# A macaron transformer block: the mixer's input projections in sets of seven block products

## The chip, the cores and the metric

One Trainium2 chip, one core. The time is the device time of one execution in microseconds (us); a profiled execution gives its span, from the first to the last instruction, on that core. The engines: PE (TensorE, matrix products), ACT (ScalarE), DVE (VectorE), POOL (GpSimd), and SP (SyncE), which issues DMA transfers. Each engine works through its own queue in order.

## The reference, cut to what matters

512 tokens, width 1024, float32 in and out.

```python
x = x + 0.5 * swiglu(rmsnorm(x, g1), w_gu1, w_down1)          # d_ff 2816
x = x + hybrid_mixer(rmsnorm(x, gm), ...)
x = x + 0.5 * swiglu(rmsnorm(x, g2), w_gu2, w_down2)
return rmsnorm(x, gf)

def hybrid_mixer(h, ...):
    cb, cc, cu, q, k, v, g_lr, r, ga, gb = split(h @ w_in)    # 3x1024, 2x512, 1024, 16, 3x1024
    y_conv = (cb * causal_short_conv(cc * cu, conv_w)) @ w_out_conv
    log_a = log_sigmoid(g_lr @ gate_w_up + gate_b) / 16
    o = gla_chunked(q, k, v, log_a)                           # 4 heads, chunks of 64 tokens
    o = o * rsqrt(mean(o * o) + eps) * gla_norm_g
    y_gla = (o * silu(r)) @ w_out_gla
    return (sigmoid(ga) * y_conv + sigmoid(gb) * y_gla) @ w_o
```

## The kernel before, in words

Activations lie transposed: 8 tiles `x[k]` of 128 features by 512 tokens. Every float32 operand of a large product is split into a rounded part h and the remainder l (type float32r), and a product is three passes on PE: h*h, h*l, l*h. A weight unit of 128 x 1024 arrives in an `f` buffer by an SP transfer (L254); ACT casts it to `wh` (L279), and DVE subtracts to get `wl` (L280). `PLAN` lists the weight units, `STEPS` their order; `Weights.take` issues casts two steps ahead of use, and `fetch` starts loads `early` steps ahead.

A plain column tile (`mm_single`, L307 to L309) is 8 k tiles x 3 passes = 24 matmuls of 512 columns. `mm_group` does four column tiles with k outermost, `mm_wide` four token tiles of v.

In both FFNs most up columns go instead by sets (`Set`, L469): two columns of 256 by 512 tokens and 1024 inputs, taken as 2 x 2 blocks, need seven block products and not eight, at the price of sums. The seven are called m1, p2, q6, p5, q7, p4, p3. Four weight units of a set are summed among themselves: one sum by DVE (L267), three by transfers that add, on POOL's queue (L258, `f<-f`). `Operands.make` builds the seven sums and differences of the normed input once per FFN, with scratch tiles `bf` and two rings, `opA` (8 tiles) and `opB` (6). Products collect in three PSUM banks a set; ACT copies the bank after m1, q6 and q7 (L474), before the next product goes into the same bank; DVE combines the results. `order` interleaves neighbouring sets.

The mixer uses no sets. It works on x times the norm's gain and scales by the norm's row at each evacuation: q and k of heads 0 and 1 (group), q and k of heads 2 and 3, then the gating of all four heads in one go (`gates`, `decays`, `qk_scale`: Abs, Exp, Ln, scan, Exp, then multiplies on DVE and POOL) around the two halves of v, then per head state and output between the 24 convolution tiles, then 8 tiles of r, 8 of ga with 8 of w_out_conv, 8 of gb with 8 of w_out_gla, and w_o. Everything lives in a pool `tp` of 50 tiles; `f` has 4 buffers there, and 10 in an FFN. As soon as `x[d]` is final, `Norm.add` splits it and adds up its squares; `Norm.finish` sums over partitions on PE (L413, L414) and makes the row.

`last_down` produces the output with tokens on partitions: 20 of 22 k tiles for all eight outputs (four token tiles by two halves), then per output the last two, followed by the residual, squares, final norm and store (L705 to L738); multiplying by the final gain is POOL's (L443 from `part`).

The order of instructions on each engine is set by a planner that goes by modelled costs and readiness; where the code says `manual_schedule` it is the order written. When a phase ends, its tiles' memory is given to the next phase's, and a new tile waits for the last use of the old ones under it.

Of the kernel before, what the change touches and what calls it, by code (L numbers as in the profile page):

```python
# [38 lines left out]
ODD_FILL = 272  # L39

# [69 lines left out]

def ffn_plan(up, down, plain, slow):
# [5 lines left out]
    firsts = []  # L117
    for s in range(plain // 2, KF // 2):
        firsts.append(len(PLAN))
        PLAN.extend((up, 4 * j, 4, (i * DFF + s * HW,), HW) for i in range(2) for j in range(2))  # L120
    STEPS.extend(order(firsts))
    units(full(down, KF))
    ENDS.append(len(STEPS))


def mixer_plan():
    units(group("w_in", KD, (QO, KO, QO + P, KO + P)))
    for h in (2, 3):
        units(single("w_in", KD, QO + h * P))
        units(single("w_in", KD, KO + h * P))  # L130
    units(wide("w_in", KD, VO))
    units(wide("w_in", KD, VO + 512))
    for j in range(KD):
        for c in (CC, CU, CB):
            units(single("w_in", KD, c + j * P))
    for j in range(KD):
        units(single("w_in", KD, RO + j * P))
    for d in range(KD):
        units(single("w_in", KD, GA + d * P))
        units(single("w_out_conv", KD, d * P))  # L140
    for d in range(KD):
        units(single("w_in", KD, GB + d * P))
# [18 lines left out]
def block_kernel(ctx: ExitStack, tc: tile.TileContext, xT, vecs, gf, gup, wgl, wts, out):  # L161
# [48 lines left out]
    X = keep.tile([P, KD, S], F32, tag="X", name="X")  # L210
    x = [X[:, k] for k in range(KD)]
    for n, b in (("wh", 3), ("wl", 3), ("opA", 8)):
        pools[n] = ctx.enter_context(tc.tile_pool(name=n, bufs=b))
    acc_row = ctx.enter_context(tc.tile_pool(name="acc_row", bufs=1))
    class Weights:
# [13 lines left out]
        def phase(self, early):  # L229
# [4 lines left out]
            for i in range(lo, self.end):  # L234
                n, p = STEPS[i]
                if p == "m1":
                    self.loads.setdefault(max(lo, i - 6), []).append(n)
# [22 lines left out]
        def issue(self):  # L260
# [16 lines left out]
            h = tile_of("wh", [P, 1024], F32R)  # L277
            l = tile_of("wl", [P, 1024], F32R)
# [58 lines left out]
    def mm_wide(mat, kt, col, ah, al):  # L337
        o = [MM() for _ in range(NTB)]
        for u in wide(mat, kt, col):
            h, l = W.take(u)  # L340
            for i in range(u[2]):
# [3 lines left out]
                for t in range(NTB):  # L345
# [4 lines left out]
                    nc.tensor.matmul(o[t], b, wh, start=False, stop=k == kt - 1)  # L350
        return o
# [8 lines left out]
    def halves(dtype):  # L360
        t = tile_of("opA", [P, 1024], dtype)
# [116 lines left out]
    class Operands:  # L478
# [3 lines left out]
        def __init__(self, b, nk):  # L482
            self.b = b
            self.nk = nk
            self.parts = {}
            self.f = {}

        def split(self, p, v):
            n = self.nk * HW
            h, l = (tile_of("opB" if p in ("m1", "p2", "q6") else "opA", [P, 1024], F32R)  # L490
                    for _ in range(2))
            hv, lv = (t[:, :n].rearrange("p (k t) -> p k t", t=HW) for t in (h, l))
# [4 lines left out]
        def new(self):  # L497
            t = tile_of("bf", [P, 1024])
            return t[:, : self.nk * HW].rearrange("p (k t) -> p k t", t=HW)

        def make(self, p):
            if p in self.parts:
                return
            b, f = self.b, self.f
            if p == "q6":
                f["D1"] = self.new()
                nc.vector.tensor_tensor(out=f["D1"], in0=b(0, 0), in1=b(0, 1), op=ALU.subtract)
                f["D2"] = self.new()
                nc.vector.scalar_tensor_tensor(out=f["D2"], in0=b(1, 1), scalar=-1.0, in1=f["D1"],
                                               op0=ALU.mult, op1=ALU.subtract)  # L510
            if p == "q7":
                f["T3"] = self.new()
                nc.vector.tensor_tensor(out=f["T3"], in0=b(1, 1), in1=b(0, 1), op=ALU.subtract)
            if p == "p4":
                f["T4"] = self.new()
                nc.vector.scalar_tensor_tensor(out=f["T4"], in0=f["D2"], scalar=-1.0, in1=b(1, 0),
                                               op0=ALU.mult, op1=ALU.subtract)
            v = {"m1": lambda: b(0, 0), "p2": lambda: b(1, 0), "q6": lambda: f["D2"],
                 "p5": lambda: f["D1"], "q7": lambda: f["T3"], "p4": lambda: f["T4"],
                 "p3": lambda: b(1, 1)}[p]()  # L520
            self.split(p, v)

# [3 lines left out]
    def run_sets(make, ahead=2):  # L526
# [6 lines left out]
        for i, n in enumerate(sets):  # L533
            sets[n] = make(i)
        for i, (n, p) in enumerate(seq):
            for n_, p_ in seq[i : i + ahead + 1]:
                sets[n_].group.make(p_)
            sets[n].run(p)


    def ffn(up, down, norm, nxt, plain, at):
# [25 lines left out]
        xo = Operands(normed, 4)  # L567
# [57 lines left out]
        def split_hid(k):  # L625

            h, l = (tile_of("opB", [P, 2, S], F32R) for _ in range(2))
# [31 lines left out]
    def natural(i):  # L659

        o = AUX()
# [4 lines left out]
    def last_down(us, split_hid):  # L666
        gr = []
        for e in range(2):
            g = tile_of("bf", [P, 1024])[:, :512]
# [12 lines left out]
        for k in range(KF - 2):  # L682
# [6 lines left out]
        w = [W.take(u) for u in us[KF - 2 :]]  # L689
        hl = split_hid(KF - 2)  # L690
# [8 lines left out]
        def part(t, e):  # L699

            s0, s1, b0, v, r, q = fin[t]
            for i in range(2):
                mm(t, e, KF - 2 + i, w[i], hl)
# [3 lines left out]
            nc.scalar.activation(blocks(T()), xt, AF.Square, accum_out=s1 if e else s0)  # L707
            y = T()
            ys[t].append(y)
            mul(blocks(y), xt, blocks(gr[e]), nc.gpsimd)  # L710
            if e == 0:
                nc.scalar.activation(b0, s0, AF.Copy, scale=1.0 / D, bias=EPS)
            else:
                nc.scalar.activation(r, s1, AF.Sqrt, scale=1.0 / D, bias=b0)

        def rstd(t):
            s0, s1, b0, v, r, q = fin[t]
            nc.vector.scalar_tensor_tensor(out=v, in0=s1, scalar=1.0 / D, in1=b0,
# [6 lines left out]
            if t != last:  # L725
                mul(r, r, q)

        def store(t, e):
            s0, s1, b0, v, r, q = fin[t]
            xt = ys[t][e]  # L730
            if t == last:
                nc.vector.tensor_scalar(out=xt, in0=xt, scalar1=r, scalar2=q,
                                        op0=ALU.mult, op1=ALU.mult)
            elif e:
                nc.vector.tensor_scalar(out=xt, in0=xt, scalar1=r, scalar2=None, op0=ALU.mult)
            else:
                nc.scalar.activation(xt, xt, AF.Copy, scale=r)
            nc.sync.dma_start(out[t, e], xt)  # L738

        with tc.manual_schedule(engines={ENG.PE, ENG.DVE, ENG.Activation, ENG.Pool}):  # L740

            early = front.tile([P, 1], F32, tag="early", name="early")
            nc.scalar.activation(early, hl[1][:, 1, 0:1].bitcast(F32), AF.Square)
            nc.scalar.activation(early, early, AF.Sqrt)
            for t in range(NTB):
# [12 lines left out]


    def mixer(norm, nxt):  # L760
        xh, xl = norm.h, norm.l
        cpool = pools["small"]

        maskf = cpool.tile([P, P], F32, tag="maskf", name="maskf")
        mask = cpool.tile([P, P], I32, tag="mask", name="mask")
        nc.gpsimd.memset(maskf, 1.0)
# [5 lines left out]
        upad = []  # L772
        for i in range(2):
            u = cpool.tile([P, S + 2], F32, tag=f"upad{i}", name=f"upad{i}")
            nc.gpsimd.memset(u[:, :2], 0.0)
            upad.append(u)
        gl_raw = cpool.tile([P, KD, RANK], F32, tag="glraw", name="gl_raw")
        nc.sync.dma_start(gl_raw, wgl)
        gl_w = cpool.tile([P, KD, 3, 2 * RANK], F32R, tag="glw", name="gl_w")
        cpool.tile([P, ODD_FILL], F32, tag="fill", name="odd_fill")  # L780
        reset = T()
        nc.gpsimd.memset(reset, 1.0)
        nc.gpsimd.memset(reset.rearrange("p (c t) -> p c t", t=CH)[:, :, 0:1], 0.0)
        sc = []
        for i in range(2):
            s = T()
            nc.gpsimd.memset(s, 0.0)
            sc.append(s)


        nc.vector.tensor_copy(gl_w[:, :, 0, :RANK], gl_raw)
        nc.vector.tensor_tensor(out=gl_w[:, :, 0, RANK:], in0=gl_raw,
                                in1=gl_w[:, :, 0, :RANK].bitcast(F32), op=ALU.subtract)
        for i in (1, 2):
            nc.gpsimd.tensor_copy(gl_w[:, :, i], gl_w[:, :, 0].bitcast(F32))
# [12 lines left out]
        def gate_k(k):  # L808
            if k == 2:
# [335 lines left out]
```

## Time and profile before

| | us |
|---|---|
| median of 3 runs (lowest, highest) | 1240.21 (1239.68, 1240.63) |
| profiled execution | 1239.92 |
| its span | 1238.2 |
| busy PE / DVE / ACT / POOL | 1219.9 / 691.0 / 493.3 / 116.9 |
| first FFN, mixer, second FFN, roughly | 0 to 352, 352 to 870, 870 to 1238 |

A line such as `L307 ... x480 | 188.3, 392 | 0.0` gives engine, operation, output and inputs, count, busy us, mean ns of one, and idle time of the engine before them with its cause. Matmuls overlap, so their mean length is not their spacing. Times in a timeline or chain are start and length from the start of the span.

### The profile page before, as it was taken

The page shows a single profiled execution, that of the slowest core. Times are in us where ns is not written, and L with a number is a line of the kernel's source. Part 1 is how long each engine was busy: PE and PEld are TensorE (multiplying, and loading weights), DVE is VectorE, ACT ScalarE, POOL GpSimd, SP SyncE. Part 2 cuts the span into 40 slices and gives each one's busy share as a digit, 9 for nine tenths or more (in the row PEclk, how much of TensorE's full clock was granted, in tenths as well). Part 3 has the DMA queues.
Part 4 walks back from the last instruction along what each step waited for, and adds up shares of the span by engine and source line. Part 5 has one row for each costly group of instructions (what it writes and reads, how often), then busy time and mean ns, then how long its engine had stood idle before and what let it go on. Part 6 is the DMA issues. An engine that isn't in the chain of part 4 may idle for free.

```text
span 1238.2 us, 16644 instructions
## 1 busy us (share of the span) xinstructions
PE 1219.9 (99%) x6874; PEld 1070.5 (86%) x6874; DVE 691.0 (56%) x817; ACT 493.3 (40%) x628; POOL 116.9 (9%) x131
## 2 busy tenths in 40 slices
PE   9999999999999999999999999999899999999996
PEld 8899999888878788888888888888689999998885
DVE  7976666532374764444584334445587656563325
ACT  6555445422252722222344222223355545452233
POOL 0011110000010251100011000000001111100003
PEclk9999999999999999999999999999899999999998
DMA  9477776631232223222223333330648777753201
GB/s 340 105 185 191 177 191 170 165 95 34 70 92 85 85 85 86 82 72 86 85 85 102 97 91 102 102 91 30 238 101 202 177 185 175 183 171 88 66 1 68
DMA packets 42748, 149.75 MB, mean 121 GB/s; under 512 B 4944, under 2 KB 5072, under 8 KB 42672
## 3 DMA queue, kind: packets, MB, share of 16 engines
q1 hardware_dynamic: 34752, 120.34, 30.5%
q0 software_dynamic: 7776, 28.32, 13.1%
q8 instruction: 54, 0.88, 0.3%
q14 instruction: 22, 0.18, 0.0%
q10 hardware_dynamic: 144, 0.03, 0.0%
HBM read 118.26 MB, written 2.10 MB: 97 GB/s over the span
## 4 chain that ended last, share of the span: by engine, by line
PE 94%; DVE 2%; ACT 1%; DMA 1%; issue 1%; POOL 0%; DVEq 0%; ACTq 0%; POOLq 0%
PE mm L469 27%; PE mm L307 14%; PE mm L308 14%; PE mm L309 14%; PE mm L331 7%; PE mm L679 2%; PE mm L678 2%; PE mm L680 2%; PE mm L349 1%; DMA f<-f 1%; PE aux L309 1%; PE aux L307 1%; PE aux L308 1%; PE mm L350 1%; PE mm L348 1%
## 5 line engine op out<-in xcount | busy, mean ns | idle before, releaser
L279 ACT CAST wh<-f 128x1024 fp32r<-128x1024 f32 (+1 forms) x275 | 287.4, 1046 | 599.0 <-PE mm L308 238.0
L280 DVE TENSOR_TENSOR wl<-f,wh 128x1024 fp32r<-128x1024 f32 (+1 forms) x275 | 337.2, 1229 | 262.3 <-ACT wh L279 260.2
L469 PE MATMUL mm<-opA,wh 128*128 128x256 f32 x1152 | 210.0, 283 | 1.3 <-ACT tp L474 1.3
L307 PE MATMUL mm<-opA,wh 128*128 128x512 f32 x480 | 188.3, 392 | 0.0
L308 PE MATMUL mm<-opA,wh 128*128 128x512 f32 x480 | 187.6, 391 | 0.0
L309 PE MATMUL mm<-opA,wl 128*128 128x512 f32 x480 | 187.0, 390 | 0.0
L469 PEld LDWEIGHTS mm<-opA,wh 128*128 128x128 f32 x1152 | 179.8, 192 | 1.8 <-ACT tp L474 1.7
L469 PE MATMUL mm<-opA,wl 128*128 128x256 f32 x576 | 163.0, 283 | 0.0
L469 PE MATMUL mm<-opB,wh 128*128 128x256 f32 x864 | 158.1, 284 | 0.0
L469 PEld LDWEIGHTS mm<-opB,wh 128*128 128x128 f32 x864 | 134.8, 192 | 0.2
L469 PE MATMUL mm<-opB,wl 128*128 128x256 f32 x432 | 122.2, 283 | 0.0
L469 PEld LDWEIGHTS mm<-opA,wl 128*128 128x128 f32 x576 | 110.6, 192 | 0.0
L309 PEld LDWEIGHTS mm<-opA,wl 128*128 128x128 f32 x480 | 90.2, 188 | 18.7
L308 PEld LDWEIGHTS mm<-opA,wh 128*128 128x128 f32 x480 | 90.1, 188 | 18.4
L307 PEld LDWEIGHTS mm<-opA,wh 128*128 128x128 f32 x480 | 90.1, 188 | 18.4
L258 POOL DMA_DIRECT2D f<-f x54 | 46.6, 863 | 603.4 <-DVE f L267 294.1
L469 PEld LDWEIGHTS mm<-opB,wl 128*128 128x128 f32 x432 | 82.9, 192 | 0.0
L443 DVE TENSOR_TENSOR tp<-mm,tp 128x512 f32<-128x512 f32 x36 | 24.8, 691 | 102.5 <-PE mm L309 101.8
L307 PE MATMUL mm<-tp,wh 128*128 128x512 f32 x160 | 62.2, 389 | 0.0
L308 PE MATMUL mm<-tp,wh 128*128 128x512 f32 x160 | 62.2, 389 | 0.0
L309 PE MATMUL mm<-tp,wl 128*128 128x512 f32 x160 | 62.2, 389 | 0.0
L678 PE MATMUL mm<-wh,opB 128*128 128x512 f32 x132 | 51.4, 389 | 0.0
(204 smaller groups left out, 1700.2 us busy)
## 6 DMA issues: line engine op xcount, KB each, us to landing
f<-wts SPq DMA_DIRECT2D x219, 512.0 KB, 3.9
f<-f POOLq DMA_DIRECT2D x54, 512.0 KB, 4.8
X<-xT SPq DMA_DIRECT2D x8, 256.0 KB, 5.3
y<-tp SPq DMA_DIRECT2D x8, 256.0 KB, 2.1
f<-wts SPq DMA_DIRECT2D x2, 256.0 KB, 3.5
bf<-gf SPq DMA_DIRECT2D x2, 256.0 KB, 4.3
tp<-gup SPq DMA_DIRECT2D x6, 32.0 KB, 1.8
gl_raw<-wgl SPq DMA_DIRECT2D x1, 64.0 KB, 4.2
```

The lines of the kernel that those rows point to most:

```text
L258: nc.gpsimd.dma_start(out_, a, accum_op=ALU.add)
L279: nc.scalar.copy(h[:, :w], raw[:, :w])
L280: nc.vector.tensor_tensor(out=l[:, :w], in0=raw[:, :w], in1=h[:, :w].bitcast(F32), op=ALU.subtract)
L307: nc.tensor.matmul(o, wh, ah, start=first, stop=False)
L308: nc.tensor.matmul(o, wh, al, start=False, stop=False)
L309: nc.tensor.matmul(o, wl, ah, start=False, stop=last)
L331: nc.tensor.matmul(o[c], w[:, s : s + P], a[k], start=k == 0 and j == 0, stop=k == kt - 1 and j == 2)
L443: (eng or nc.vector).tensor_tensor(out=out_, in0=a, in1=b, op=ALU.mult)
L469: nc.tensor.matmul(to, ww[:, s], aa[:, t], start=fresh and k == 0 and e == 0 and j == 0, stop=k == 3 and j == 2, skip_group_check=True)
L678: nc.tensor.matmul(o[t][e], a, wh, start=k == 0, stop=False)
L679: nc.tensor.matmul(o[t][e], a, wl, start=False, stop=False)
L680: nc.tensor.matmul(o[t][e], b, wh, start=False, stop=k == KF - 1)
```

## The change

1. **Mixer by sets.** cc, cu, cb, r, ga and gb (48 column tiles) become 12 sets; q, k and v stay plain, in the order group, half of v, q and k of heads 2 and 3, other half of v. The input is multiplied by the norm's gain and row in place (`normed`), so nothing is scaled at evacuation.
2. **Heads one at a time.** Gating, scores, state, output and squares of heads 0 and 1 run between the plain tiles, of 1 to 3 in hooks between products of the first six sets. All of it is on PE, ACT and DVE; POOL no longer multiplies.
3. **Memory.** x goes to DRAM at the mixer's start and returns near its end; the gates, after Sigmoid, go to DRAM by transfers on ACT's queue and return by SP's. Buffers `f`: 10 in all phases; `tp`: 6 in the mixer, 9 in an FFN.
4. **One ring** `op` of 14 tiles replaces `opA`, `opB` and `bf`; the operand sums are formed in place, one after the other (m1, p2, p5, q6, q7, p4, p3). The last two tiles of w_o are both multiplied before either is evacuated.
5. **Tail.** The last four k tiles (`TAIL`) are taken output by output; POOL's multiply moves to DVE, one store of the last tile to ACT's queue.

```diff
+TAIL = 4
+MSETS = [("ga", 0), ("gb", 0), ("conv", 0), ("ga", 1), ("conv", 1), ("gb", 1), ("conv", 2),
+         ("conv", 3), ("cb", 0), ("cb", 1), ("r", 0), ("r", 1)]
...
     units(group("w_in", KD, (QO, KO, QO + P, KO + P)))
+    units(wide("w_in", KD, VO))
     for h in (2, 3):
         units(single("w_in", KD, QO + h * P))
         units(single("w_in", KD, KO + h * P))
-    units(wide("w_in", KD, VO))
     units(wide("w_in", KD, VO + 512))
-    for j in range(KD):
-        for c in (CC, CU, CB):
-            units(single("w_in", KD, c + j * P))
-    for j in range(KD):
-        units(single("w_in", KD, RO + j * P))
+    base = {"ga": GA, "gb": GB, "cb": CB, "r": RO}
+    sets("w_in", [(CC + i * HW, CU + i * HW) if n == "conv" else
+                  (base[n] + 2 * i * HW, base[n] + (2 * i + 1) * HW) for n, i in MSETS])
...
-    for n, b in (("wh", 3), ("wl", 3), ("opA", 8)):
+    for n, b in (("wh", 3), ("wl", 3), ("op", 14)):
...
+            late = at >= len(STEPS) - TAIL
+            h = tile_of("op" if late else "wh", [P, 1024], F32R)
+            l = tile_of("op" if late else "wl", [P, 1024], F32R)
...
+        hooks = {
+            (0, "m1"): [lambda: scores(1)], (0, "q6"): [lambda: state(1)],
+            (0, "q7"): [lambda: output(1)], (0, "p4"): [lambda: squares(1)],
+            (0, "p3"): [move],
+            (1, "q6"): [lambda: gates(2)], (1, "q7"): [decays], (1, "p4"): [lambda: scale(2)],
+            (2, "q6"): [lambda: scores(2)], (2, "q7"): [lambda: state(2)],
+            (2, "p4"): [lambda: output(2)], (3, "q6"): [lambda: squares(2)],
+            (3, "q7"): [lambda: gates(3)], (3, "p3"): [decays], (4, "q6"): [lambda: scale(3)],
+            (4, "p3"): [lambda: scores(3)], (5, "q6"): [lambda: state(3)],
+            (5, "p4"): [lambda: output(3)], (5, "p3"): [lambda: squares(3)],
+        }
...
+                gates_d[name][d : d + 2, :, half(l)].rearrange("e p t -> p e t"), pair(t))
...
+        def gate(name, d):
+            t = T()
+            nc.sync.dma_start(t, gates_d[name][d])
+            return t
...
-        for d in range(4, KD):
+        for d in range(4, KD - 2):
             evac(d, mm_single("w_o", KD, d * P, m_h, m_l))
+        for d, o in [(d, mm_single("w_o", KD, d * P, m_h, m_l)) for d in range(KD - 2, KD)]:
+            evac(d, o)
...
-    FFN = dict(f=10, opB=6, hid=11, bf=2, tp=6)
+    FFN = dict(f=10, hid=11, tp=9)
...
-    with phase("small2", f=4, small=1, tp=50):
-        W.phase(2)
+    with phase("small2", f=10, tp=6, v=4, qk=2, g=1, y=4, small=1):
+        W.phase(4, 5)
```

In the new tail, `part(t, e, acc)` does the four k tiles of an output, its residual, squares and gain; `rstd(t)` and `store(t)` follow a token tile later:

```diff
-        for k in range(KF - 2):
+        for k in range(KF - TAIL):
...
-            for i in range(2):
-                mm(t, e, KF - 2 + i, w[i], hl)
+            for i in range(TAIL):
+                mm(t, e, KF - TAIL + i, w[i], hl[i // 2])
...
-            mul(blocks(y), xt, blocks(gr[e]), nc.gpsimd)
+            mul(blocks(ys[t][e]), xt, blocks(gr[e]))
...
+            (nc.scalar if t == last else nc.sync).dma_start(out[t, 1], ys[t][1])
```

More of the change, by code (lines that the diff above doesn't have):

```diff
@@ L116, in ffn_plan @@
         units(single(up, KD, DFF + f * P))
[L117 to L121, printed above, removed]
+    sets(up, [(s * HW, DFF + s * HW) for s in range(plain // 2, KF // 2)])
     units(full(down, KF))
@@ L495, in split, with run_sets @@
             self.parts[p] = (h, l)
[L497 to L521, printed above, removed]
         def get(self, p):
             return self.parts[p]
-    def run_sets(make, ahead=2):
+    def run_sets(make, ahead=2, hooks={}):
         at = W.taken
@@ L532, in run_sets @@
         sets = {n: None for n, _ in seq}
-        for i, n in enumerate(sets):
+        number = {n: i for i, n in enumerate(sets)}
+        for n, i in number.items():
             sets[n] = make(i)
@@ new lines, in mixer, with normed @@
+        for h in range(2):
+            evac_q(h, qk[2 * h])
+            evac_k(h, qk[2 * h + 1])
+        X = XS[-1]
+        done_k = set()
+        def normed(j, l):
+            for k in range(4 * j, 4 * j + 4):
+                if k not in done_k:
+                    done_k.add(k)
+                    nc.vector.scalar_tensor_tensor(
+                        out=x[k], in0=x[k], scalar=vec[:, norm.goff + k : norm.goff + k + 1],
+                        in1=row, op0=ALU.mult, op1=ALU.mult)
+            return X[:, 4 * j : 4 * j + 4, l * HW : (l + 1) * HW]
@@ new lines, in v_half, with one, extra @@
+        def v_half(i, extra=None):
+            for t, o in enumerate(mm_wide("w_in", KD, VO + 512 * i, xh, xl, extra)):
+                nc.scalar.copy(vt[i][t], o)
+        def one(fs):
+            def extra(k):
+                for f in fs.get(k, ()):
+                    f()
+            return extra
+        v_half(0, one({1: [lambda: gates(0)], 3: [decays], 5: [lambda: scale(0)]}))
+        oq = mm_single("w_in", KD, QO + 2 * P, xh, xl)
+        scores(0)
+        evac_q(2, oq)
+        ok = mm_single("w_in", KD, KO + 2 * P, xh, xl)
@@ new lines, in mixer, with move @@
+        state(0)
+        evac_k(2, ok)
+        xo.make("m1")
+        oq = mm_single("w_in", KD, QO + 3 * P, xh, xl)
+        output(0)
+        evac_q(3, oq)
+        ok = mm_single("w_in", KD, KO + 3 * P, xh, xl)
+        squares(0)
+        gates(1)
+        evac_k(3, ok)
+        xo.make("p2")
+        v_half(1, one({1: [decays], 3: [lambda: scale(1), lambda: xo.make("p5")],
+                       5: [lambda: xo.sum("q6")]}))
+        OB = []
+        def move():
+            OB.append(big("O").rearrange("p (h e) t -> p h e t", e=2))
+            for h in range(2):
+                nc.scalar.copy(OB[0][:, h], O[h])
+            for h in range(HEADS):
+                O[h] = OB[0][:, h]
+            for i in range(4):
+                nc.gpsimd.memset(Y[i][:, :, :2], 0.0)
@@ new lines, in cb_done, with done @@
+        def cb_done(i):
+            def done(s, p):
+                bank, v = s.bank, s.v
+                y = [Y[2 * i + a][:, :, 2:] for a in range(2)]
+                if p == "p4":
+                    c = y[1][:, :, half(0)]
+                    nc.vector.scalar_tensor_tensor(out=c, in0=pair(bank["b"]), scalar=-1.0, in1=c,
+                                                   op0=ALU.mult, op1=ALU.mult)
+                    return
+                t = quarter(s, p)
+                if t is not None:
+                    c = y[p == "q7"][:, :, half(p != "p2")]
+                    mul(c, pair(t), c)
+            return done
@@ new lines, in r_done, with use, f, make @@
+        def r_done(i):
+            def use(a, l, t):
+                def f():
+                    o = O[2 * i + a][:, :, half(l)]
+                    mul(o, o, pair(t))
+                late.append(f)
+            return act_done(AF.Silu, use)
+        kinds = {"ga": lambda i: gate_done("ga", i), "gb": lambda i: gate_done("gb", i),
+                 "conv": conv_done, "cb": cb_done, "r": r_done}
+        def make(n):
+            name, i = MSETS[n]
+            f = kinds[name](i)
+            def done(s, p):
+                if p in ("p2", "p5", "q7", "p4", "p3"):
+                    finish_late()
+                f(s, p)
+            return Set(xo, done)
@@ L1052, in mixer @@
+        c_h, c_l = parts([Y[i][:, :, 2:] for i in range(4)])
+        m = [two(d // 2)[:, d % 2] for d in range(KD)]
+        n64 = [front.tile([P, HEADS * 16], F32, tag=t, name=f"{t}o") for t in
+               ("st_v", "st_s", "st_r")]
+        r64, s64, q64 = n64
+        newton_rsqrt(r64, vs, s64, q64)
+        og = []
         for d in range(KD):
-            gp = mm_single("w_in", KD, GA + d * P, xh, xl)
-            t = T()
-            mul(t, gp, row)
-            nc.scalar.activation(t, t, AF.Sigmoid)
+            t = gate("ga", d)
```

569 lines of the change are left out of this document (309 added, 260 removed).

## The prediction

> **What bounds the kernel now.** I read the page first: busy shares (part 1), then the chain that ended last by engine (part 4).
>
> ```profile
> span 1238.2 us, 16644 instructions
> PE 1219.9 (99%) x6874; PEld 1070.5 (86%) x6874; DVE 691.0 (56%) x817; ACT 493.3 (40%) x628; POOL 116.9 (9%) x131
> ...
> PE 94%; DVE 2%; ACT 1%; DMA 1%; issue 1%; POOL 0%; DVEq 0%; ACTq 0%; POOLq 0%
> ```
>
> PE is busy 99% and carries 94% of the chain. So this change can win in three ways only: less matmul time, shorter holes in PE, a shorter end after PE. The sum goes against the profiled execution: 1239.92 us, its span of 1238.2 and 1.7 around it; the median of the runs, 1240.21, is 0.3 above.
>
> **Matmul time.** The chain in order of time merges unbroken stretches, so it gives rates, where a group's mean gives overlapping lengths: first 96 matmuls of 512 columns, then the 168 of one set of 256 columns.
>
> ```profile
> 826.89 21.76 PE mm L331 x96
> ...
> 1009.88 20.15 PE mm L469 x168
> ```
>
> Four column tiles cost 96 plain matmuls (8 k tiles, 3 passes): 21.76 us, 0.2267 each. The same columns as a set are 7 products of 4 k tiles, 2 halves, 3 passes: 168 matmuls, 20.15 us, 0.1199 each. A set saves 1.61 us (7%, not 1/8, as 256 columns cost more than half of 512). 48 tiles make 12 sets: **-19.3 us**. Other matmuls stay in number: q, k, v, the three output projections, the attention. That all of this time is on the path is shown by the windows: in the mixer PE lacks 1.3 us of 518.4.
>
> ```profile
> core 0: us, PE busy (x) PEld busy (x) DVE busy (x) ACT busy (x) POOL busy (x), PEclk, DMA share, GB/s
> 30.00:50.00 20.00, 20.00 (x90) 16.55 (x89) 19.88 (x33) 9.94 (x12) 1.73 (x2) 1.00 0.29 66
> 351.90:870.30 518.40, 517.07 (x2355) 426.74 (x2353) 267.25 (x336) 173.44 (x231) 56.90 (x55) 1.00 0.29 86
> 401.00:447.00 46.00, 45.27 (x200) 36.68 (x198) 35.41 (x37) 30.33 (x52) 20.81 (x22) 1.00 0.29 84
> 447.10:487.20 40.10, 40.10 (x199) 33.31 (x198) 18.27 (x23) 10.37 (x13) 8.63 (x10) 1.00 0.29 88
> 874.00:902.00 28.00, 27.69 (x112) 22.08 (x113) 16.48 (x25) 10.49 (x11) 0.89 (x1) 0.89 0.68 242
> 1009.88:1030.03 20.15, 20.15 (x170) 20.15 (x170) 12.49 (x13) 9.88 (x14) 2.58 (x3) 1.00 0.75 173
> ```
>
> A rule to weigh here: the Trainium skill, "TensorE: Matmul & The Clock Gate", section "Back-to-back issue gap", gives a warm gap of the column count over 2.4 GHz plus 2.5 ns. By it a set would be 18.3 us against 20.7, the saving 28.5 us in all and the result 1204 (estimates from that page). The trace disagrees by about 11 ns a matmul at both widths, so I keep 19.3.
>
> **The hole ahead of the second FFN.** From the timeline and SP's waits:
>
> ```profile
> 870.02 0.39 PE L309 MATMUL mm<-tp,wl 128*128 128x512 f32 x1
> 874.04 0.80 PE L413 MATMUL aux<-tp,ones_r 128*128 128x512 f32 x1 [3.63 <-ACT tp L356]
> ...
> 875.35 2.13 PE L663 MATMUL aux<-ident,X 128*128 128x128 f32 x8
> ...
> 869.58 2.30 SPq L254 DMA_DIRECT2D f<-wts  x5
> ...
> SPq L254 <- PE mm L308: 29.9, 1, 29.9
> ...
> 876.67 2.92 ACT L279 CAST wh<-f 128x1024 fp32r<-128x1024 f32 x3
> 877.75 23.11 PE mm L331 x96
> ...
> 5.75 16.70 PE mm L331 x72
> 22.44 0.23 PE aux L413
> 22.91 5.46 PE mm L331 x24
> ```
>
> PE's last w_o matmul issues at 870.02, the first FFN2 matmul at 877.75. The idle row names ACT (the split of the norm's squares), but SP tells the cause: FFN2's first weight loads sat 29.9 us for a matmul of the mixer, whose tiles lie where those load buffers lie (f=4 in the mixer, 10 in an FFN). Then the group ran 1.35 us slow (23.11 against 21.76; clock 0.89 in that window). The change declares f=10 in all three phases, first in each, so a load should wait only for an earlier load buffer, long free. PE then needs, from 870.25: 21.76, two sums (0.23 each as in the last rows) and 8 transposes (0.44 per four by the chain row below), 23.1 us, against 900.86-870.25 = 30.6: **-7.5**. Next late would be k tiles 6 and 7 of the norm, which the change evacuates after both last w_o products, and the norm's sum; they are used 6 x 2.72 = 16 us into the group. The first FFN runs so already (last three rows): 72 matmuls, the sum at the sixth k tile, 24 more, no hole. The bounds: 0 (it waits for something else) and -7.5.
>
> **The tail.** After PE's last matmul:
>
> ```profile
> 1071.21 0.44 PE aux L663 x4
> ...
> 1227.14 0.39 PE L680 MATMUL aux<-wh,opB 128*128 128x512 f32 x1
> ...
> 1227.82 2.60 POOL L443 TENSOR_TENSOR tp<-X,bf 128x512 f32<-128x512 f32 x2 [1.13 <-DVE X L705]
> 1228.00 0.68 DVE L705 SCALAR_TENSOR_TENSOR X<-aux,X 128x512 f32<-128x512 f32 x1
> 1229.33 1.11 DVE L721 SCALAR_TENSOR_TENSOR fin<-fin 128x1 f32<-128x1 f32 x1
> ...
> 1231.55 0.61 ACT L707 ACTIVATE tp<-X 128x512 f32<-128x512 f32 x1
> 1233.07 0.22 DVE L721 SCALAR_TENSOR_TENSOR fin<-fin 128x1 f32<-128x1 f32 x1
> 1233.57 1.00 DVE L732 TENSOR_SCALAR tp<-tp,fin 128x512 f32<-128x512 f32 x2
> ```
>
> PE ends at 1227.14+0.23 = 1227.37, 10.8 us before the span does. VectorE is behind: two tiles (128 tokens each) are still to be evacuated, and its one-column operation takes 1.11 us beside POOL's multiplies, 0.22 without them. With four k tiles per output PE gives a token tile every 2 x 12 x 0.2267 = 5.44 us, and VectorE's work per tile without POOL, 2 x (0.68 + 0.68) for evacuations and gain, five one-column operations at 0.22 and one scaling at 0.5, 4.3 us, keeps up. What remains after PE: one evacuation (0.7), the squares to the first final multiply as now (1231.55 to 1233.57, 2.0) less 0.5 of POOL's drag and plus a small multiply (0.2), the last scaling (about 1.0), then landing and closing as now (1238.2-1234.57 = 3.6): about 7.1: **-3.7**. The four late weight units and the operands lie in 12 of 14 ring slots and are cast during the k tiles before; bounds -1 and -4.5.
>
> **What the set stage adds.** Prices:
>
> ```profile
> L280 DVE TENSOR_TENSOR wl<-f,wh 128x1024 fp32r<-128x1024 f32 (+1 forms) x275 | 337.2, 1229 | 262.3 <-ACT wh L279 260.2
> L279 ACT CAST wh<-f 128x1024 fp32r<-128x1024 f32 (+1 forms) x275 | 287.4, 1046 | 599.0 <-PE mm L308 238.0 <-issue 139.1 <-PE mm L469 112.9
> L968 DVE SCALAR_TENSOR_TENSOR tp<-tp,d,aux 128x256 f32<-128x256 f32 x8 | 3.8, 480 | 3.7 <-PE aux L962 3.6
> PE mm L469 <- ACT tp L474: 1.3, 2, 0.9
> f<-f POOLq DMA_DIRECT2D x54, 512.0 KB, 4.8
> L258 POOL DMA_DIRECT2D f<-f x54 | 46.6, 863 | 603.4 <-DVE f L267 294.1 <-DVE wl L280 270.2 <-DVE st_q L437 24.7
> 404.15 1.39 ACT L853 ACTIVATE tp<-aux,vec 128x512 f32<-128x512 f32 x2 [1.34 <-PE aux L849]
> 405.56 1.28 ACT L859 ACT_TABLE_LOAD   x1
> 406.86 2.19 ACT L859 ACTIVATE tp<-tp 128x512 f32<-128x512 f32 x4
> 409.07 1.28 ACT L861 ACT_TABLE_LOAD   x1
> ```
>
> A set of the FFN takes 12.49 us of VectorE and 9.88 of ScalarE in its 20.15 (window 1009.88:1030.03), three more weight units than a plain quadruple. The mixer's sets are alike (a gate set less two evacuations, a conv set plus four taps). On top come the heads, 2.5 of them inside the first six sets. A head's gating costs VectorE (35.41 - 9 x 1.23)/4 = 6.1 (window 401:447), state and output some 3, and the six half-size multiplies that leave POOL, at 0.48, 2.9: 12 us. Preparing the block operands adds some 12 once. The first six sets: 75 + 30 + 12 = 117 of VectorE in 6 x 20.15 + 2.5 x 7.5 (a head's PE time: 40.10 less six tiles of 24 x 0.2267) = 140 us of PE, 84%. That by itself is no stall: at 30:50 VectorE is busy 19.88 of 20 and PE all 20. In-order waits are: where the gating runs now, PE lost 0.73 us (401:447). I take that for each head in the sets and the two before, plus 0.9 for the end of the sets (the longest wait for the bank copies there) and some for their start: **+3.5**. Bounds 0 and 24 (first rival). ScalarE also issues 16 gate stores, which hold no other engine; gates return on SP's queue during the output projections, each 256 KB load ahead of a weight load that is due four units (4 x 5.44 us) later: 0. x goes to memory and back on POOL's queue (16 issues at about 0.9 us, with no weight sum due then or 54 us before use): 0. The scaling by the norm's row, dropped from the evacuations, was beside PE: 0. The gate weights' duplicates, now made by VectorE and not POOL, end a PE wait of 0.6 or renew it: 0, bounds +-1.
>
> **Sum:** -19.3 - 7.5 - 3.7 + 3.5 = -27.0; 1239.9 - 27.0 = **1213**.
>
> **The rivals.**
> First: ScalarE eats the gain. The gating runs for one head at a time: three table loads for each (Exp, Ln as in the rows, Exp again for the decays), where now one of each serves four heads, and Sigmoid's table after. In a row a head is 0.7 + 3 x (1.28 + 0.6) + 1.6 = 8 us of ScalarE. A product lasts 2.88, and the next product into the same bank may start only when ScalarE has copied the bank. If nothing is slipped between, a copy comes 5 us late; at one or two places for each of the heads, 8 to 24 us, say 12: 1225. For it: ScalarE is in order. Against it: with all four heads in one run, 401:447, PE lost 0.73. The Trainium skill, "ScalarE: Activation LUTs", section "What ACT_TABLE_LOAD costs", adds a drain of 1380 ns to each load, and its rule is to batch by table set; with it this rival would be some 4 us a head dearer (estimate). The trace shows no drain: the load starts at 405.56, 0.02 us after the activations before it, and the next follows 0.02 after the load.
> Second: the f buffers do not free FFN2's loads, or PE waits there for the norm instead: 7.5 comes back, 1220.5. For it: the row that PE names is the norm's.
> Third, slower: the weight sums come late. Each set needs a11 + a21, issued on POOL's queue after m1's cast and due at q6's, four products (11.5 us) on. Cast 1.05, difference 1.23, issue 0.86 and landing 4.8 make 7.9; with the lead of two products on the cast (5.8 - 2.3) there are 7.1 us to spare. In gate sets stores join DMA engines that are 75% busy. It decides when landing takes 14.2 us, not 4.8: then 12 sets lose 2.25 each and the gain is gone. At 15 us: 37 us lost, 1250. Against it: 4.8 was measured at that 75%.
>
> **How the numbers follow.** Forecast (1207 to 1219) 0.58; first rival (1219 to 1238) 0.22; second (1217 to 1224) 0.10; third 0.06; more gain than summed, below 1207, 0.02; more than one rival, 0.02. The 1204 that follows from the Trainium skill's "TensorE: Matmul & The Clock Gate" would lie in that 0.02. The range 1206 to 1231 leaves out the upper half of the first, the third and the low end. Faster by over 0.2% (2.5 us, about what a measurement tells from no change) has 0.89, within it 0.03, slower 0.08.
>
> **What would show it.** Right: L469-like stretches of 168 in about 20.2 us in the mixer, FFN2's group following w_o with no idle row and a granted clock of 1.00, 7 us from PE's last matmul to the end. Wrong: waits of PE for bank copies above 5 us in all (first rival), SP's first FFN2 load waiting again (second), the weight casts waiting for the f<-f transfers (third).

## The result, and the profile after

| | before | after |
|---|---|---|
| median (lowest, highest), us | 1239.95 (1239.5, 1240.63) | 1212.78 (1210.31, 1213.22; 4 runs) |
| profiled execution / its span, us | 1239.92 / 1238.2 | 1210.31 / 1208.6 |

Ratio 0.9776, 95% interval 0.9759 to 0.9793: 27.2 us less between the medians, where 27.0 were forecast (1213.0). The profiled execution of after is the shortest of its four, 2.1 to 2.9 us below the others; what those others have on top is shown below. One run of the kernel e9 (1302.2 us, at a granted clock of 0.848) is left out of its median and range.

The page of after, the lines that answer to the first ones shown of before:

```profile
span 1208.6 us, 18730 instructions
PE 1196.6 (99%) x7738; PEld 1095.3 (91%) x7738; DVE 768.5 (64%) x923; ACT 579.5 (48%) x718; POOL 89.7 (7%) x125
...
PE 97%; ACT 1%; DVE 1%; issue 0%; DMA 0%; DVEq 0%
```

PE bounds it still, with more of the chain than before; VectorE and ScalarE each do some 80 us more, beside it. The stages show where the 29.6 us between the two spans went. First before, in windows cut where PE ends the first FFN, the mixer, the first group of the second FFN (FFN2) and its last matmul:

```profile
core 0: us, PE busy (x) PEld busy (x) DVE busy (x) ACT busy (x) POOL busy (x), PEclk, DMA share, GB/s
0.00:351.91 351.91, 350.43 (x2255) 321.76 (x2255) 213.21 (x240) 160.71 (x194) 26.26 (x41) 1.00 0.57 153
351.91:870.25 518.34, 517.01 (x2355) 426.74 (x2353) 267.24 (x336) 173.43 (x231) 56.90 (x55) 1.00 0.29 86
870.25:900.86 30.61, 26.71 (x108) 21.13 (x108) 17.38 (x27) 11.22 (x13) 0.89 (x1) 0.89 0.74 258
900.86:1227.37 326.51, 325.57 (x2161) 300.87 (x2159) 186.66 (x202) 144.04 (x182) 28.86 (x31) 1.00 0.51 128
1227.37:1238.20 10.83, 0.16 (x1) 0.00 (x0) 6.47 (x16) 3.89 (x11) 3.99 (x3) 0.69 0.38 145
```

The same five stages of after, and below them the stretch from the first set to the last head's squares, some six and a half sets:

```profile
0.00:351.04 351.04, 349.76 (x2255) 321.42 (x2256) 213.38 (x239) 160.63 (x194) 28.65 (x45) 1.00 0.58 165
351.04:853.11 502.07, 498.22 (x3219) 453.80 (x3219) 345.37 (x433) 261.81 (x327) 37.84 (x53) 1.00 0.56 155
853.11:875.36 22.25, 22.25 (x99) 18.40 (x99) 12.58 (x21) 8.15 (x10) 0.89 (x1) 1.00 0.37 107
875.36:1201.55 326.19, 326.19 (x2168) 301.71 (x2167) 194.44 (x224) 147.17 (x186) 22.35 (x26) 1.00 0.49 129
1201.55:1208.60 7.05, 0.16 (x1) 0.00 (x0) 2.73 (x8) 1.74 (x4) 0.00 (x0) 0.83 0.39 149
...
450.93:610.08 159.15, 155.30 (x1248) 150.98 (x1248) 107.74 (x133) 106.67 (x138) 16.53 (x21) 1.00 0.69 177
```

By stage: first FFN -0.9, mixer 518.34 to 502.07 = -16.3, FFN2's first group 30.61 to 22.25 = -8.4, the rest of FFN2 -0.3, the end after PE 10.83 to 7.05 = -3.8. Sum -29.6. The -0.9 of the first FFN is no gain of the change: the profiles of after and of the experiments that leave that FFN as it is in after end it between 351.04 (after) and 352.45 (e5), and before's 351.91 lies within. In the mixer PE's busy time falls by 18.8 and its idle time rises by 2.5 (from 1.33 to 3.85); all 3.85 lie in the last row, where the heads run between products of sets. The chain of work, in the mixer's sets and around FFN2's first group:

```profile
610.08 112.44 PE mm L485 x937
...
809.59 21.76 PE mm L345 x96
...
853.11 16.33 PE mm L345 x72
...
869.90 5.46 PE mm L345 x24
```

96 plain matmuls still take 21.76 us, and 937 matmuls of the mixer's sets 112.44, which is 20.16 for a set's 168. FFN2 runs as the first FFN does: 72 matmuls, the norm's two sums, 24 more, no hole, and a granted clock of 1.00 instead of 0.89. The eight transposes that lay in the hole run later, from 922.9 on, between sets. SP's loads from 800 to 860 us wait now for VectorE's differences, which read earlier load buffers, and not for a matmul of the mixer:

```profile
SPq L267 <- DVE wl L294: 54.7, 7, 21.4
```

**The waits that came.** PE's waits in after, by releaser (total, times, longest):

```profile
PE mm L485 <- DVE wl L294: 2.5, 1, 2.5
...
PE aux L957 <- DVE qk L459: 0.8, 1, 0.8
PE mm L485 <- ACT wh L293: 0.5, 1, 0.5
```

None is for a bank copy. The 2.5 and the 0.5 are one place: the weights of a product at 552.6. PE, VectorE and ScalarE there, from the timeline:

```profile
552.62 0.50 PE L485 MATMUL mm<-op,wh 128*128 128x256 f32 x2 [0.48 <-ACT wh L293]
555.66 0.38 PE L485 MATMUL mm<-op,wl 128*128 128x256 f32 x1 [2.53 <-DVE wl L294]
...
551.19 0.69 DVE L914 TENSOR_TENSOR g<-g,g 128x512 f32<-128x512 f32 x1 [4.42 <-ACT g L913]
551.92 1.22 DVE L915 TENSOR_TENSOR_SCAN g<-reset,g 128x512 f32<-128x512 f32 x1
...
554.39 1.22 DVE L294 TENSOR_TENSOR wl<-f,wh 128x1024 fp32r<-128x1024 f32 x1
...
545.34 1.28 ACT L912 ACT_TABLE_LOAD   x1
...
547.28 1.28 ACT L1164 ACT_TABLE_LOAD   x1
548.58 0.63 ACT L1164 ACTIVATE tp<-tp 128x512 f32<-128x512 f32 x1
549.23 1.28 ACT L913 ACT_TABLE_LOAD   x1
...
550.52 0.64 ACT L913 ACTIVATE g<-g 128x512 f32<-128x512 f32 x1
...
551.52 1.05 ACT L293 CAST wh<-f 128x1024 fp32r<-128x1024 f32 x1
```

Read back from the matmul: its remainder waits for VectorE, which waited 4.42 us for head 3's gating (L913) on ScalarE, where the Sigmoid of a gate set (L1164) fell between the gating's Exp and Ln. Each change of function is a table load of 1.28 us, and the weights' cast stands behind them. The cast is done at 552.57, yet the remainder is begun at 554.39: in VectorE's queue the gating's scan and decays, late by the same wait, stand before it. The Trainium skill, "ScalarE: Activation LUTs", section "Table sets: the hidden batching unit", would batch calls by table set, and this stretch bears that out. The drain of 1380 ns a load that the Trainium skill states in the same page's section "What ACT_TABLE_LOAD costs" is not in these rows: the Sigmoid starts 0.02 us after its load has ended, the next load 0.02 us after the Sigmoid.

**What the other runs have on top.** Windows of 5 us behind that wait (columns as above), in a second profile of after (e8), and from its chain the first matmuls of the mixer and of FFN2:

```profile
555.00:560.00 5.00, 3.33 (x18) 3.33 (x19) 4.48 (x5) 4.95 (x6) 0.86 (x1) 0.73 0.17 56
560.00:565.00 5.00, 5.00 (x41) 5.00 (x41) 2.45 (x4) 3.35 (x7) 0.00 (x0) 0.93 1.01 219
...
352.05 9.97 PE mm L345 x44
...
855.60 16.33 PE mm L345 x72
```

PE's waits in the mixer are the same, but the granted clock drops behind it, to 0.73 and 0.93 in these windows (1.00 throughout in the first profile). The span is 1211.0, 2.4 more: 1.0 stands already at the mixer's start (352.05, in after 351.04), and the mixer takes 503.55 against 502.07, 1.5 more. In e12, which has the same mixer and dropped to 0.50 and 0.82, it takes 504.39, 2.3 more. The mean clock of after's runs is 0.999 in the shortest and 0.995 in the three others, of which there is no profile.

**The end.** The timeline of after from PE's last matmul:

```profile
1201.32 0.39 PE L702 MATMUL aux<-op,op 128*128 128x512 f32 x1
1201.75 0.69 DVE L726 SCALAR_TENSOR_TENSOR X<-aux,X 128x512 f32<-128x512 f32 x1 [0.84 <-PE aux L702]
1202.47 0.63 ACT L728 ACTIVATE tp<-X 128x512 f32<-128x512 f32 x1 [1.38 <-DVE X L726]
...
1204.39 0.72 ACT L754 ACTIVATE tp<-tp,fin 128x512 f32<-128x512 f32 x1 [0.87 <-DVE fin L459]
```

One evacuation is left when PE ends, not two; 1.92 us from the squares to the last scaling, 0.72 for it, 3.5 to close.

### The profile page after: what moved, and what is told of

Same layout as the page of the kernel before. It is cut to its first block, busy times and chain, and to the rows that moved or that the text cites. A ratio compares the mean times of both kernels' runs of the same rounds, so it can differ in the third digit from the quotient of the medians.

```text
span 1208.6 us, 18730 instructions
## 1 busy us (share of the span) xinstructions
PE 1196.6 (99%) x7738; PEld 1095.3 (91%) x7738; DVE 768.5 (64%) x923; ACT 579.5 (48%) x718; POOL 89.7 (7%) x125
## 3 DMA queue, kind: packets, MB, share of 16 engines
q1 hardware_dynamic: 36912, 124.27, 29.6%
## 4 chain that ended last, share of the span: by engine, by line
PE 97%; ACT 1%; DVE 1%; issue 0%; DMA 0%; DVEq 0%
PE mm L485 49%; PE mm L322 7%; PE mm L321 7%; PE mm L323 7%; PE mm L345 7%; PE mm L701 2%; PE mm L700 2%; PE mm L702 2%; PE mm L362 1%; PE mm L364 1%; PE mm L363 1%; PE aux L322 1%; PE aux L701 1%; PE aux L321 1%; PE aux L702 1%; PE aux L700 1%
## 5 line engine op out<-in xcount | busy, mean ns | idle before, releaser
L485 PE MATMUL mm<-op,wh 128*128 128x256 f32 x3360 | 608.0, 284 | 0.5 <-ACT wh L293 0.5
L485 PEld LDWEIGHTS mm<-op,wh 128*128 128x128 f32 x3360 | 523.8, 191 | 1.6 <-ACT wh L293 0.7
L485 PE MATMUL mm<-op,wl 128*128 128x256 f32 x1680 | 476.6, 284 | 2.5 <-DVE wl L294 2.5
L485 PEld LDWEIGHTS mm<-op,wl 128*128 128x128 f32 x1680 | 321.4, 191 | 2.8 <-DVE wl L294 2.7
L321 PE MATMUL mm<-op,wh 128*128 128x512 f32 x388 | 151.5, 390 | 0.0
L323 PE MATMUL mm<-op,wl 128*128 128x512 f32 x388 | 151.3, 390 | 0.0
L322 PE MATMUL mm<-op,wh 128*128 128x512 f32 x388 | 151.1, 389 | 0.0
L323 PEld LDWEIGHTS mm<-op,wl 128*128 128x128 f32 x388 | 72.9, 188 | 15.1
L321 PEld LDWEIGHTS mm<-op,wh 128*128 128x128 f32 x388 | 72.9, 188 | 15.1
L322 PEld LDWEIGHTS mm<-op,wh 128*128 128x128 f32 x388 | 72.9, 188 | 14.9
L345 PE MATMUL mm<-op,wh 128*128 128x512 f32 x256 | 63.5, 390 | 0.2 <-DVE op L396 0.2
L345 PEld LDWEIGHTS mm<-op,wh 128*128 128x128 f32 x256 | 48.0, 188 | 10.5 <-issue 0.3
L490 ACT COPY tp<-mm 128x512 f32<-128x512 f32 x90 | 52.1, 579 | 2.8 <-PE mm L485 2.7
L700 PE MATMUL mm<-wh,op 128*128 128x512 f32 x108 | 42.1, 390 | 0.0
L701 PE MATMUL mm<-wl,op 128*128 128x512 f32 x108 | 42.1, 390 | 0.0
L702 PE MATMUL mm<-wh,op 128*128 128x512 f32 x108 | 42.1, 389 | 0.0
L280 DVE TENSOR_TENSOR f<-f,f 128x1024 f32<-128x1024 f32 x30 | 36.7, 1224 | 0.8
L345 PE MATMUL mm<-op,wl 128*128 128x512 f32 x128 | 34.3, 390 | 0.0
```

The costliest lines, as they stand in the source:

```text
L321: nc.tensor.matmul(o, wh, ah, start=first, stop=False)
L322: nc.tensor.matmul(o, wh, al, start=False, stop=False)
L323: nc.tensor.matmul(o, wl, ah, start=False, stop=last)
L345: nc.tensor.matmul(o[c], w[:, s : s + P], a[k], start=k == 0 and j == 0, stop=k == kt - 1 and j == 2)
L485: nc.tensor.matmul(to, ww[:, s], aa[:, t], start=fresh and k == 0 and e == 0 and j == 0, stop=k == 3 and j == 2, skip_group_check=True)
L490: nc.scalar.copy(v, o)
```

## The experiments

The theory (A): the sum's own terms. Sets save what their rows say, the hole was the `f` buffers, the tail was VectorE's backlog, the added waits were ScalarE's order. Each edit is against after unless it says otherwise; times are medians (lowest to highest) beside 1212.78, ratios against before with their intervals.

**e1, fewer sets.** Seven of the first FFN's nine sets as plain column tiles.

```diff
-PLAIN1, PLAIN2 = 4, 4
+PLAIN1, PLAIN2 = 18, 4
```

> The changed kernel, but seven of the nine sets of the first FFN are taken as 28 plain column tiles (nothing left out). Theory A, rates of the chain (a set 20.15 us, four plain tiles 21.76): +7 x 1.61 = +11.3 us, about 1224 against the changed kernel's 1212.8. Theory B, the skill's gap of columns over 2.4 GHz plus 2.5 ns (18.3 against 20.7, estimate): +16.6 us, about 1229. Theory C, sets win by relieving other engines and not by matmul time: less than +5 us.

1223.31 (1222.92 to 1224.0), ratio 0.9865 (0.9849 to 0.9882): +10.5, 1.5 a set, by the rows 1.61. The 16.6 that follows from the Trainium skill's "TensorE: Matmul & The Clock Gate", section "Back-to-back issue gap" (which states that gap for an isolated matmul), and the small figure of theory C both fall. Sets are worth the same in an FFN and in the mixer.

**e2, the hole back.** FFN2's first five loads wait for the mixer's last output tile.

```diff
+            if self.hold is not None:            # x[KD - 1], for FFN2's first loads
+                nc.vector.tensor_copy(t[:, :1], self.hold[:, :1])
             nc.sync.dma_start(t[:, :w], wts[o
...
```

> The changed kernel, but the first five weight loads of the second FFN are made to wait for the last x tile of the mixer: VectorE first writes one column of each load buffer from it. Theory A (the hole ahead of FFN2 came from loads that waited, and 7 to 8 us were won by freeing them): a hole of 6 to 7 us of PE comes back after the last w_o matmul, the group behind it runs at a clock below 1, total +7 to +9 us, about 1220 to 1222. Theory B (PE waited for the norm, or the gain there came from the group's order): under +2 us.

1219.49 (1217.93 to 1221.72), ratio 0.9834 (0.9819 to 0.9849): +6.7, just under what was expected. From the last w_o matmul to FFN2's first, 5.6 us pass (7.5 in before). PE's longest wait is again put down to the norm's split, as in before (3.63 there), though only the loads were touched (and five copies of one column added on VectorE); the clock behind it drops too:

```profile
PE aux L432 <- ACT tp L375: 3.6, 1, 3.6
...
850.00:860.00 10.00, 6.42 (x27) 4.76 (x25) 5.15 (x12) 3.10 (x5) 0.00 (x0) 0.95 0.23 72
```

So the loads were the cause; that a row names ACT says only which of PE's operations stood first in its queue.

**e3, the tail at two k tiles** (`TAIL = 2`).

> The changed kernel with two k tiles per output in the tail and not four; the multiply by the final gain stays on VectorE. A token tile then takes PE 2.7 us and VectorE 4.3, so VectorE falls behind by 1.6 us a tile over three tiles: the end after PE is 7.0 + 3 to 5 = 10 to 12 us, total +3 to +5 us. Rival (POOL's multiply alone had made the old tail long): 7 to 8 us after PE, total under +1 us.

1217.62 (1215.77 to 1217.86), ratio 0.9814 (0.98 to 0.9829): +4.8. PE's last matmul:

```profile
1203.76 0.39 PE L702 MATMUL aux<-op,op 128*128 128x512 f32 x1
```

It ends at 1203.99, the span at 1215.9: 11.9 after PE, against 7.05. With two k tiles the multiply on VectorE is no gain at all: before, with two and the multiply on POOL, had 10.83.

**e4 and e12, the final gain's multiply on POOL.** In e4 for all four token tiles, in e12 for the first three.

```diff
-            mul(blocks(ys[t][e]), xt, blocks(gr[e]))
+            mul(blocks(ys[t][e]), xt, blocks(gr[e]), nc.gpsimd)   # e12: nc.vector if t == last else nc.gpsimd
...
-        with tc.manual_schedule(engines={ENG.PE, ENG.DVE, ENG.Activation}):
+        with tc.manual_schedule(engines={ENG.PE, ENG.DVE, ENG.Activation, ENG.Pool}):
```

> The changed kernel with four k tiles per output, but POOL does the multiply by the final gain again. If the four k tiles are enough to keep VectorE ahead even at 1.1 us per one-column operation beside POOL: the end after PE grows only by POOL's longer last multiply (1.4 against 0.7) and the drag, +1 us at most. Rival (POOL's drag is what made the old tail long): +3 us or more, as VectorE's operations beside POOL go from 0.2 to 1.1 us in every tile.

> The final-gain multiply goes to POOL for the first three token tiles and stays on DVE for the last. With it on POOL for all four, 3.67 us passed from PE's last matmul to the last scaling (3.56 without), but 5.7 from there to the end of the span (3.4 to 3.5 without). Theory A: what is late is the closing, because POOL still had a multiply within the last 8 us: without it the closing is 3.4 to 3.5 again and the time 1212 to 1214. Theory B: the closing is long because the last phase's end takes in POOL at all, wherever its multiplies stand: 5.7 again and 1215 to 1216.

e4: 1215.66 (1214.19 to 1216.34), ratio 0.98 (0.9785 to 0.9815): +2.9, a miss. e12: 1212.97 (1212.62 to 1213.3), ratio 0.9784 (0.9771 to 0.9798): no change. The last scaling of e4, and of e12:

```profile
1205.53 0.63 DVE L734 SCALAR_TENSOR_TENSOR fin<-fin 128x1 f32<-128x1 f32 x1 [0.79 <-ACT tp L728]
...
1206.96 0.72 ACT L754 ACTIVATE tp<-tp,fin 128x512 f32<-128x512 f32 x1 [1.14 <-DVE fin L459]
```

```profile
1206.74 0.72 ACT L754 ACTIVATE tp<-tp,fin 128x512 f32<-128x512 f32 x1 [0.87 <-DVE fin L459]
```

From the start of the last evacuation to that of the last scaling it is 2.91 us in e4 (from 1204.05) and 2.64 in after (from 1201.75): VectorE lost 0.3 us beside POOL, in the row above (0.63, in after 0.16). (The 3.67 beside 3.56 in e12's expectation takes PE's end by two measures; by one it is 3.83 beside 3.56.) But e4's span ends at 1213.4, 5.7 after that scaling has ended, and e12's at 1210.9, 3.4 after. A multiply of POOL in the last token tile lengthens the closing. Why stays open: in e4 POOL's last multiply ended 1.5 us before the last scaling did (1204.88 + 1.26), in before 1.6 (1231.56 + 1.38), and there the closing was 3.6.

PE's last matmul ends at 1203.85 in e4, so 9.5 us remain after it. The four ends together: 10.8 with two k tiles and POOL (before), 11.9 with two and VectorE (e3), 9.5 with four and POOL (e4), 7.05 with four and VectorE (after). Neither step brings the whole of the tail's gain alone.

**e5 and e6, the gating moved.** A conv set goes between the two gate sets, and head 3's gating, with what follows it, up to a set later; e6 also moves scores, state, output and squares one product on.

```diff
-MSETS = [("ga", 0), ("gb", 0), ("conv", 0), ("ga", 1), ...
+MSETS = [("ga", 0), ("conv", 0), ("gb", 0), ("ga", 1), ...
...
-            (3, "q7"): [lambda: gates(3)], (3, "p3"): [decays], (4, "q6"): [lambda: scale(3)],
...
+            (4, "q6"): [lambda: gates(3)], (4, "q7"): [decays], (4, "p4"): [lambda: scale(3)],
...
```

> The changed kernel with conv 0 as the second set and the gating of head 3 moved from sets 3 and 4 to sets 4 and 5, so that each head's Abs, Exp, Ln, Exp runs inside a convolution set, which uses no Sigmoid (nothing left out). Theory A (the 3 us in which PE waits for weights at 552 us, and the half clock that follows it in most runs, come from ScalarE switching between Exp's, Ln's and Sigmoid's tables seven times in 15 us): that wait is gone, PE's waits in the mixer are under 1.5 us, no granted clock below 1 before the tail, 1206 to 1209. Theory B (VectorE's and ScalarE's plain load does it): the wait moves with the gating, 1211 to 1214.

> As the kernel before it, and scores, state, output and squares of heads 2 and 3 each one product later. Theory A: it also takes away the 0.8 us in which PE waits for the scaled q and k of head 2: 0 to 1 us less than the kernel before it. Theory B: no change, as PE's other work moves with it.

e5: 1209.27 (1208.76 to 1209.99), ratio 0.975 (0.9737 to 0.9764): -3.5, and a mean clock of 0.998 or 0.999 in every run. Table loads fall from 29 to 23. I had expected PE's waits in the mixer to fall under 1.5 us in all; the cast's and the q/k wait are gone, but 2.5 for remainders are left, in three pieces:

```profile
PE mm L485 <- DVE wl L294: 2.5, 3, 1.1
```

No single wait is above 1.1, and the granted clock is 1.00 in every window from 450 to 610. The mixer takes 500.02 us (352.45 to 852.47), against 502.07 in after's first profile, without the drop, and 503.55 in e8, with it: some 2 us of the gain are there even against the mixer without the drop, the rest is the drop. e6: 1209.41 (1208.69 to 1209.74), ratio 0.9751 (0.9738 to 0.9765): nothing; the q/k wait of 0.8 that it aimed at had gone with e5 already, so it told nothing apart.

**e7, no Sigmoid table.** The gates' Sigmoid is replaced by a copy; the function is left out of the result.

> The changed kernel with the gates' Sigmoid replaced by a plain copy (the gates are left without their function), order unchanged; two or three of the seven table loads around 545 to 560 us go. Theory A (tables): the wait of 3 us and the low clock behind it go, 1206 to 1209. Theory B (load): the wait stays at 2 us or more, 1210 to 1213.

1207.39 (1206.66 to 1207.8), ratio 0.9735 (0.9722 to 0.9748): -5.4. The stretch that has the heads in after:

```profile
450.93:610.08 159.15, 158.88 (x1278) 154.80 (x1278) 109.56 (x137) 96.45 (x133) 16.91 (x22) 1.00 0.71 181
```

PE lost 0.3 us there instead of 3.85, with no less work on VectorE (109.56, in after 107.74) and the table loads down from 29 to 18: the tables are the cause, not the amount of work on VectorE or the transfers. The q/k wait of 0.8 went as well. In after a Sigmoid's table load, at 498.71, stands between the two Exp of head 2's gating ahead of it.

**e8, after once more, on the chip of e5 to e7.** 

> The changed kernel unaltered, beside the three above on one chip. Theory A: its runs stand 3 to 6 us above the two that rearrange the gating, with the mean granted clock at 0.995 in most; theory B: within 1.5 us of them.

1212.99 (1211.66 to 1214.68), ratio 0.9782 (0.9768 to 0.9795): the 3.6 to 5.6 us by which e5 to e7 stand below it are theirs, not the chip's. Its mean clocks are 0.994 to 0.998, not 0.995 in most.

**e9 and e10, more weight sums.** In the mixer's sets a11 + a21 by two, then three adding transfers in a row (so the sum is another): the third rival's price.

```diff
-                self.add(a11, a21)
+                for _ in range(2 if ENDS[0] <= at < ENDS[1] else 1):   # e10: 3
+                    self.add(a11, a21)
```

> The changed kernel, but in the mixer's sets the transfer that adds a21 to a11 on POOL's queue runs twice, one after the other (the sums are then wrong by one a21). Theory A (third rival's account: 7.1 us to spare, and one more issue and landing cost 0.9 + 4.9 = 5.8): nothing waits, within 1.5 us of the changed kernel, 1211 to 1214. Theory B (DMA engines, 70% busy already, or the queue, leave less room): casts wait for f<-f, +1 us or more a set, 1225 or more.

> The same transfer three times over (sums wrong by two a21). Theory A: 11.6 us more against 7.1 to spare, so each set's q6 comes 4 to 5 us late: 12 x 4.5 = +54 us, 1250 to 1275, the weight casts waiting for f<-f. Theory B (the planner moves the sums earlier, so the room is larger than 7.1): under +10 us.

e9: 1220.22 (1217.67 to 1222.54), ratio 0.9846 (0.9826 to 0.9866), +7 to +9: above A's bound, below the rival's. e10: 1265.87 (1263.55 to 1266.7), ratio 1.0202 (1.0186 to 1.0217): +53, the number that A had. In e9 one set of twelve ran out of room; PE, ScalarE's cast, and the two issues on POOL's queue:

```profile
709.57 0.50 PE L486 MATMUL mm<-op,wh 128*128 128x256 f32 x2 [2.25 <-ACT wh L293]
710.83 0.39 PE L486 MATMUL mm<-op,wl 128*128 128x256 f32 x1 [0.76 <-DVE wl L294]
...
708.47 1.99 ACT L293 CAST wh<-f 128x1024 fp32r<-128x1024 f32 x2 [4.94 <-DMA f<-f]
...
695.80 0.86 POOL L271 DMA_DIRECT2D f<-f  x1 [6.42 <-DVE wl L294]
703.83 0.86 POOL L271 DMA_DIRECT2D f<-f  x1 [7.17 <-DMA f<-f]
```

The second add goes out 8.03 us after the first, when that has landed, where issue and landing as I had them (0.86 + 4.8) make 5.66; it lands in turn when the cast starts, at 708.47. The sum is then complete 12.67 us after the first issue, 7.0 later than reckoned for one add, and PE waits 2.25 + 0.76. So 7.0 more is 3.0 too much: the spare there was 4.0, not 7.1. In the twelve sets the second add goes out 4.8 to 8.0 us after the first; in the eleven others PE waits for no sum. PE's waits for weights are 3.1 us above after's, and the granted clock drops behind this one too (a mean of 0.98 from 609 to 721). PE's waits in e10:

```profile
PE mm L486 <- ACT wh L293: 21.6, 9, 7.4
PE mm L486 <- DVE wl L294: 7.6, 9, 2.5
PE aux L1014 <- ACT tp L373: 5.3, 3, 2.5
```

Waits 34.5 against 3.0 is +31; the mean clock of 0.981 against 0.999, times the span of 1261.8, is another 23 (an estimate). A had put all 54 us down to waits, so its mechanism is there (casts wait for the sums), but its number fits by luck.

**e11, the best version.** e6, and `scale` cut in two parts one product apart, so that the weights' difference is not queued behind all its multiplies.

```diff
-            (1, "p4"): [lambda: scale(2)],
+            (1, "p4"): [lambda: scale_a(2)], (1, "p3"): [lambda: scale_b(2)],
...
-            (4, "p4"): [lambda: scale(3)],
+            (4, "p4"): [lambda: scale_a(3)], (4, "p3"): [lambda: scale_b(3)],
```

> The kernel with the gating in convolution sets and scores one product later, and the nine multiplies by the decays in two parts, one product apart (nothing left out). Theory A (PE's two remaining waits of 1.1 us are weights queued on VectorE behind those multiplies): they shrink below 0.4 us each and the time falls by 1.5 to 2.5 us, to about 1207. Theory B (VectorE is short of time there altogether): the same waits, 1209.

1206.16 (1205.99 to 1206.76), ratio 0.9724 (0.971 to 0.9739): 6.6 below after, with all the work, and some 3 below e6, more than the 1.5 to 2.5 expected. What is left of PE's waits for weights, and the same stretch:

```profile
PE mm L485 <- DVE wl L294: 0.2, 1, 0.2
...
450.93:610.08 159.15, 159.15 (x1286) 155.54 (x1285) 107.66 (x134) 101.74 (x135) 17.42 (x22) 1.00 0.71 182
```

PE is busy in all 159.15 us. The added waits are gone without leaving anything out, and VectorE does as much as in after (107.66), so they were order, not load.

## Why the prediction was right

- **Matmul time, -19.3.** PE's busy time in the mixer fell by 18.8; e1 prices a set at 1.5.
- **The hole, -7.5.** Measured -8.4: the group needed 22.25, not 23.1, because the eight transposes left it. That 0.9 is moved and not won: the rest of FFN2 has 0.6 more PE work (326.19 against 325.57). It is shorter all the same, by 0.3, because a wait of PE of 0.9 for a bank copy there is gone. e2 brought 6.7 back by holding up the loads, so the second rival falls.
- **The tail, -3.7.** Measured -3.8, and by its own steps: 0.9 for the evacuation, 1.92 to the last scaling (1.7 reckoned), 0.72 (1.0), 3.5 (3.6). What I had put down to POOL was off: its drag on VectorE after PE was 0.3 in e4, not 0.5, and its cost in the closing (2.3) I had not seen.
- **The added waits, +3.5.** The size was right (idle time +2.5 in the profiled run, and 1.5 to 2.3 more by the clock in e8 and e12), the place was not. I had spread it, 0.73 at each head and 0.9 for bank copies; 3.0 of the 3.85 are one wait, for weights behind three table loads, 0.8 is for head 2's q and k, and none is for a bank copy. The waits of before, 1.33, went: 0.6 for the gate weights' duplicates and 0.7 in v. The new ones are the first rival's mechanism, Sigmoid between the gating's tables (e7), at two places, through VectorE and the cast instead of the copy. So the term was near by luck: its size was taken from waits of another kind. VectorE's load was reckoned too high as well: 107.74 us in the 159.15 of the heads' stretch, 68% and not 84%.
- **The third rival.** One sum lands in time everywhere, as forecast, but the spare that I worked out, 7.1, was 4.0 in the tightest set (e9). There a landing of 4.8 + 4.0 + 2.25 = 11 us, not 14.2, would cost what a set gains.
- **The agreement of 27.2 and 27.0 is closer than the terms.** The sum was made for the profiled execution, which came out at 29.6 less; the other runs took 2 to 3 us longer, in e8's profile by 1.5 for the clock's drop and 1.0 ahead of the mixer. The 2.6 between 27.0 and 29.6 are the hole and the first FFN (0.9 each; the latter differs by more than that between executions), the mixer (0.5), the rest of FFN2 (0.3) and the tail (0.1).

## What to carry to other kernels

When PE is busy nearly all the time, add up a change by stages in which PE's work and its idle time stand apart; each of the four terms here could then be tested by an edit of a few lines. Before you slip a function of ScalarE between products, look at which table loads it adds: three close together held up a cast and VectorE behind it. Moving the gating (e5) and letting the weights' difference in between VectorE's multiplies (e11) gave back 6.6 us. Where an idle row names an engine, ask whether a transfer's buffer stands behind it: e2 shows the same row with nothing but loads delayed.

## What the runs showed of the hardware that was not expected

- The wait of PE of 0.5 + 2.5 us, which after and seven of the experiments have in the same place, was followed by a lower granted clock in seven of these eight profiles (0.50 to 0.84 in the 5 us behind it) and not in after's. It cost the mixer 1.5 us in e8 and 2.3 in e12, half as much as the wait and more. Waits of 1.1 us apart from each other (e5) were not followed by one.
- Two adding transfers, the second behind the first on one queue, went out 4.8 to 8.0 us apart in e9's twelve sets; the group's median from issue to landing is 5.0.
- A multiply on POOL in the last token tile went with a closing 2.3 us longer (e4, 5.7 us, against 3.4 in e12, where the last multiply is VectorE's); before, which has one there too, closes in 3.6.
